# Feature-major units of a streamed gated block: 512-column products with the high weights, halves added when a unit leaves PSUM

## The chip, the core and the metric

One core of a Trainium2 chip runs the whole program. Its engines are PE (TensorE, matrix products), DVE (VectorE), ACT (ScalarE), POOL (GpSimd) and SP (SyncE, which here only issues transfers); 16 DMA engines move data between device memory and SBUF. Matrix results land in PSUM. The metric is the device time of one execution in microseconds (us), less is better.

## The reference

All arrays are float32. `x` is [1, 256, 2048]: 256 tokens with 2048 features; the branches are W = 1024 wide.

```python
h = rmsnorm(x, norm_pre)
(q_a, f_a, i_a, z_a, u_b, z_b, rkvwa_c, z_c, xbc_d, dt_d, z_d, gate_pre) = h @ w_in   # [2048, 21648]
o_a = hgrn2(q_a, f_a, i_a) * silu(z_a)
o_b = s5(u_b, ...) * silu(z_b)          # ends with g * sigmoid(g @ w_glu + b_glu), g = gelu(y)
o_c = rwkv7(token_shift(rkvwa_c), ...) * silu(z_c)
o_d = mamba2(conv4(xbc_d), dt_d, z_d)   # causal convolution over 4 tokens, per channel; silu(z) inside
merged = sum(sigmoid(gate_pre[b] + gate_bias[b]) * (o[b] @ w_up[b]) for b in range(4))
out = x + rmsnorm(merged @ w_out, norm_post)
```

The token shift is `xs + mu * (previous token's xs - xs)`. Each branch holds a recurrence over the 256 tokens (S5's is a complex scan per state). The work is mostly the three large products with `w_in`, `w_up` and `w_out`.

## The kernel before

**The stream.** The weights of all large products pass through the core once, in 444 chunks of 128 x 1024 elements (512 KB). A chunk is loaded as `raw` by a transfer on SP's queue (three raw buffers), then split in two parts of the reduced type fp32r: `hi` is a rounded copy made by ACT, `lo` is `raw - hi`, made by DVE (four buffers of each). A product of two float32 matrices is then three products of parts: high by high, high by low and low by high. The normalised input `h` lies transposed as eight tiles `h0` to `h7`; for one k tile (128 features of the contraction) there are 512 columns, 0:256 the high part of the 256 tokens and 256:512 their low part. The split of a chunk runs three chunks ahead of its products.

**Units.** A unit is a set of chunks that fill one PSUM tile `pg` of [128, 2, 512], of which there are two. In a feature-major unit (kind "fm") a 128 x 128 weight tile is the stationary operand and `h` moves past it: the result has features on the partitions and 256 tokens in a row, two feature tiles `f` to a unit. Each k tile and feature tile takes three products of 256 columns, `hi` with the high part, `hi` with the low part, `lo` with the high part, all added into the same 256 columns `ps[:, f, 0:256]`. In a token-major unit (kind "tm") the activations are stationary and 512 columns of weights move; the change does not touch it. Feature-major are `u` (chunks 0 to 15), dt (16, 17), the convolution's input xBC (18 to 49), the two low-rank inputs (50, 51), k, r, v (52 to 99), q, f (100 to 131), z of the RWKV branch (212 to 227) and of S5 (324 to 339), and the glu product of S5 (380 to 387, whose moving operand `ghl` is S5's own result). The gates, up projections and the output (388 to 443) are token-major.

**Evacuation.** When a unit's last products are issued, a generator (`shift_done`, `conv_done`, `plain_done`, `u_done`, `zfm_done`, `glu_done`, `dt_done`) takes the result out of PSUM in stages: for the token shift ACT copies the tile scaled by `mu` to `evm` and DVE combines `pg` with it; for the convolution ACT scales the tile once and DVE adds three shifted multiples of it, six reads of `pg` in all; `plain_done` (q, f) is one copy on ACT and a store on ACT's queue.

**The order.** Each engine works through its instructions in the order in which the program emits them, fixed when it is built. `_Stream.loop` emits, for each step, a split, a load, one chunk's products, stages of evacuations, and then as many stages of branch work ("jobs": S5's tiles `s50` to `s57`, the halves of HGRN, RWKV's and Mamba's steps) as fit. How many fit is settled by an estimate: each helper (`mm`, `act`, `tt`, `stt`, `ts`) books a cost on its engine's clock (`t_pe`, `t_act`, `t_dve`), and `run_jobs` goes on

```python
        while max(K.t_dve, K.t_act) <= K.t_pe + AHEAD:
```

with AHEAD = 3.7 us. A stage of a job comes only after the estimate has its last stage finished (`can`). If a unit needs a job that is not done when its products are due, `products` calls `finish`, which emits the rest of that job in one go, ahead of the unit. The glu units need job "b" (gelu of S5's early tiles read back) and "s57", S5's last tile, which has two halves; in a half, DVE computes a phase `ph`, ACT its sine and cosine `cs5`, PE the input products `pb`, DVE the rotated inputs `ta`, four scans and the products `ta`, `tb` with the cosines, and PE the output products.

**The start.** `prologue` holds x in tiles of 128 tokens by 1024 features (`x00`, `x01` the first 128 tokens, `x10`, `x11` the others), scales them by the rows' norms in pieces of 512 features, transposes them on PE into `pb` banks, and DVE and ACT write `h0` to `h7`. Products of the first two chunks (`j < 2`) come by part, as far as `h` is there.

Of the kernel before, what the change touches and what calls it, by code (L numbers as in the profile page):

```python
# [60 lines left out]
PE_GAP = 0.0  # L61
# [5 lines left out]
# the functions that each activation table serves  # L67
# [6 lines left out]
class _Kern:  # L74
    """Pools, constants and instruction helpers shared by the weight stream and the branches."""

    def __init__(self, ctx, tc, drams):
# [20 lines left out]
        self.soft = False  # L98
        self.o = {}
# [23 lines left out]
    def wait(self, n):  # L123
        """Until n more slots are free."""
# [5 lines left out]
    def wait_banks(self, n):  # L130
        """Until n more PSUM banks are free."""
# [5 lines left out]
    def fm(self, name, n=2):  # L137
        """A feature-major [128, 4 n, 256] array, in tiles of four feature tiles."""
# [23 lines left out]
    def book(self, engine, cost, out, ins):  # L162
        """Book an instruction: it starts when the engine is free and its operands are there."""
# [31 lines left out]
    def act(self, out, in_, func, **kw):  # L195
# [7 lines left out]
        ins = [in_] + [x for x in (kw.get("scale"), kw.get("bias")) if hasattr(x, "tensor")]  # L203
        self.book("t_act", cost, out, ins)
# [4 lines left out]
    def _dve(self, out, ins, ns):  # L209
        """Book a vector instruction; one that reads the last one's output waits for it."""  # L210
        self.book("t_dve", 0.06 + ns * 1e-3, out, ins)
# [15 lines left out]
    def stt(self, out, in0, scalar, in1, op0, op1, **kw):  # L227
        self._dve(out, (in0, in1), self._n(out) * 1.045)
        return self.nc.vector.scalar_tensor_tensor(out=out, in0=in0, scalar=scalar, in1=in1, op0=op0, op1=op1, **kw)  # L229

    def ts(self, out, in0, s1, s2, op0, op1=None):
        self._dve(out, (in0,), self._n(out) * 0.53)
# [21 lines left out]
    def mm(self, out, lhsT, rhs, start=True, stop=True, **kw):  # L254
        n = self._n(rhs)
        if rhs.dtype == F32R:
            cost = n * 0.427e-3 if n >= 256 else n * 1.67e-3
        else:
            cost = max(n * 1.67e-3 * min(out.shape[0], 128) / 128, 0.027)
        self.book("t_pe", cost + PE_GAP * (1 if rhs.dtype == F32R else 2), out, (lhsT, rhs))  # L260
        return self.nc.tensor.matmul(out, lhsT, rhs, start=start, stop=stop, **kw)  # L261

    def tr(self, out, in_, b=0):
        """out = in_ transposed; in_ starts at partition b."""
# [12 lines left out]
    def ld(self, out, in_):  # L277
        """A transfer whose source may still be under way."""
# [3 lines left out]
    def ldx(self, out, in_):  # L282
        """A load of what has long been in DRAM."""
# [5 lines left out]
    def st(self, out, in_):  # L289
        """A store of what the scalar engine has just written."""  # L290
# [11 lines left out]
    def split(self, hi, lo, src):  # L302
        """src (float32 in SBUF) as the exact sum of two float32r parts."""
# [3 lines left out]
    def rstd(self, out, ss, n, eps):  # L307
        """out = 1 / sqrt(ss / n + eps), small tiles."""
# [1980 lines left out]
```

## Time and profile before

| what | value |
|---|---|
| runs | 1427.38, 1429.43, 1424.73 us; median 1427.38 |
| the profiled execution | span 1427.8 us from the first to the last instruction, taken as its time |
| mean granted TensorE clock | 0.993 of full speed |
| busy, share of the span | PE 97%, PE's weight loads 86%, DVE 73%, ACT 58%, POOL 11% |
| transfers | 288.62 MB, 202 GB/s over the span |
| matmul records | 9751 |
| largest groups | splits `lo` on DVE, 444 of 1223 ns; splits `hi` on ACT, 444 of 1055 ns; feature-major products on PE, 2624 with `hi` and 1312 with `lo`; token-major products, 1408 with `hi` and 704 with `lo` against `h` |

The busy time of PE is that of pipelined products, whose durations overlap: the mean of one can be twice the pace at which they follow each other. The pace is read from a stretch of the chain of waits in which PE waits for nothing. The rows `pg<-h,hi` and `pg<-h,lo` are the feature-major products, `pg<-hi,h` and `pg<-lo,h` the token-major ones, since the stationary operand is named last.

### The profile page before, as it was taken

The page shows a single profiled execution, that of the slowest core. Times are in us where ns is not written, and L with a number is a line of the kernel's source. Part 1 is how long each engine was busy: PE and PEld are TensorE (multiplying, and loading weights), DVE is VectorE, ACT ScalarE, POOL GpSimd, SP SyncE. Part 2 cuts the span into 40 slices and gives each one's busy share as a digit, 9 for nine tenths or more (in the row PEclk, how much of TensorE's full clock was granted, in tenths as well). Part 3 has the DMA queues.
Part 4 walks back from the last instruction along what each step waited for, and adds up shares of the span by engine and source line. Part 5 has one row for each costly group of instructions (what it writes and reads, how often), then busy time and mean ns, then how long its engine had stood idle before and what let it go on. Part 6 is the DMA issues. An engine that isn't in the chain of part 4 may idle for free.

```text
span 1427.8 us, 24645 instructions
## 1 busy us (share of the span) xinstructions
PE 1390.9 (97%) x9751; PEld 1223.2 (86%) x9751; DVE 1038.0 (73%) x1422; ACT 827.1 (58%) x1136; POOL 162.0 (11%) x268
## 2 busy tenths in 40 slices
PE   8999989989999999999999999999999999999997
PEld 7999989989989887888789888888789987888886
DVE  6787488778786784576787699767978788576655
ACT  5455445845456546765578765787556444544442
POOL 6232310010025320011100001000010000000000
PEclk9999999999999999999999999999999999999999
DMA  7878985487657876477876567655686856676664
GB/s 214 239 240 263 279 270 163 135 191 232 206 155 175 228 236 179 142 203 201 232 207 198 181 207 197 211 177 172 193 197 194 214 177 191 213 267 194 183 195 135
DMA packets 199040, 288.62 MB, mean 202 GB/s; under 512 B 12453, under 2 KB 116750, under 8 KB 198926
## 3 DMA queue, kind: packets, MB, share of 16 engines
q1 hardware_dynamic: 169614, 237.15, 54.2%
q0 software_dynamic: 25216, 43.05, 13.9%
q10 hardware_dynamic: 4096, 6.86, 1.4%
q8 instruction: 76, 1.25, 0.3%
q14 instruction: 38, 0.31, 0.1%
HBM read 268.33 MB, written 18.66 MB: 201 GB/s over the span
## 4 chain that ended last, share of the span: by engine, by line
PE 71%; DMA 8%; DVE 8%; issue 6%; ACT 6%; POOL 0%; SPq 0%; ACTq 0%; DVEq 0%; POOLq 0%
PE pg L261 63%; PE pb L261 6%; DMA raw<-in_w_in_dram 6%; DVE lo L216 4%; ACT hi L207 2%; PE pb L267 1%; DVE ta L216 1%; ACT L207 1%; DMA cn<-in_s_c_im_dram 1%; DMA x<-in_x_dram 1%; DVE invtmp L216 0%; ACT hT L207 0%; DVE tb L243 0%; DVE tb L216 0%; DMA ds5b<-bl 0%
## 5 line engine op out<-in xcount | busy, mean ns | idle before, releaser
L216 DVE TENSOR_TENSOR lo<-raw,hi 128x1024 fp32r<-128x1024 f32 x444 | 541.1, 1223 | 350.6 <-ACT hi L207 342.3
L207 ACT ACTIVATE hi<-raw 128x1024 fp32r<-128x1024 f32 x444 | 465.9, 1055 | 532.7 <-PE pg L261 249.1
L261 PE MATMUL pg<-h,hi 128*128 128x256 f32 x2624 | 480.8, 286 | 4.1 <-DVE ev L229 3.6
L261 PE MATMUL pg<-hi,h 128*128 128x512 f32 x1408 | 448.1, 393 | 0.1
L261 PEld LDWEIGHTS pg<-h,hi 128*128 128x128 f32 x2624 | 409.9, 192 | 10.7 <-issue 6.9
L261 PE MATMUL pg<-h,lo 128*128 128x256 f32 x1312 | 371.6, 285 | 5.0 <-DVE lo L216 4.1
L261 PEld LDWEIGHTS pg<-hi,h 128*128 128x128 f32 x1408 | 264.9, 188 | 58.5 <-issue 2.5
L261 PE MATMUL pg<-lo,h 128*128 128x512 f32 x704 | 275.5, 391 | 2.6 <-DVE lo L216 2.4
L261 PEld LDWEIGHTS pg<-h,lo 128*128 128x128 f32 x1312 | 251.0, 192 | 6.7 <-DVE lo L216 5.4
L261 PE MATMUL pg<-hi,o 128*128 128x512 f32 x512 | 164.2, 394 | 0.0
L261 PEld LDWEIGHTS pg<-lo,h 128*128 128x128 f32 x704 | 132.6, 188 | 30.5 <-DVE lo L216 4.5
L261 PEld LDWEIGHTS pg<-hi,o 128*128 128x128 f32 x512 | 96.1, 188 | 21.9 <-issue 1.6
L261 PE MATMUL pg<-lo,o 128*128 128x512 f32 x256 | 99.8, 390 | 0.0
L261 PE MATMUL pg<-hi,mhl 128*128 128x512 f32 x224 | 71.1, 391 | 0.0
L280 POOL DMA_DIRECT2D gb<-in_gate_bias_dram x16 | 8.7, 545 | 541.1 <-DVE gate L216 477.9
L207 ACT ACT_TABLE_LOAD x51 | 65.4, 1283 | 5.3 <-DVE mss L235 2.8
L261 PEld LDWEIGHTS pg<-lo,o 128*128 128x128 f32 x256 | 48.1, 188 | 9.5
L261 PEld LDWEIGHTS pg<-hi,mhl 128*128 128x128 f32 x224 | 42.1, 188 | 8.7
L261 PE MATMUL pg<-lo,mhl 128*128 128x512 f32 x112 | 43.6, 389 | 0.0
L243 DVE TENSOR_TENSOR_SCAN tb<-s5p,ta 128x256 f32<-128x256 f32 x64 | 41.7, 701 | 0.1
L261 PEld LDWEIGHTS pg<-lo,mhl 128*128 128x128 f32 x112 | 21.0, 188 | 4.2
L261 PE MATMUL pg<-ghl,hi 128*128 128x256 f32 x128 | 23.1, 283 | 0.0
(371 smaller groups left out, 1362.6 us busy)
## 6 DMA issues: line engine op xcount, KB each, us to landing
raw<-in_w_in_dram SPq DMA_DIRECT2D x340, 512.0 KB
raw<-in_w_up_dram SPq DMA_DIRECT2D x64, 512.0 KB
raw<-in_w_out_dram SPq DMA_DIRECT2D x32, 512.0 KB
us<-duhl POOLq DMA_DIRECT2D x16, 256.0 KB, 6.4
bs<-ds5b POOLq DMA_DIRECT2D x16, 256.0 KB, 7.6
gb<-in_gate_bias_dram POOLq DMA_DIRECT2D x16, 256.0 KB, 4.7
raw<-in_s_w_glu_dram SPq DMA_DIRECT2D x8, 512.0 KB
x<-in_x_dram SPq DMA_DIRECT2D x4, 512.0 KB
```

The costliest lines, as they stand in the source:

```text
L207: return self.nc.scalar.activation(out=out, in_=in_, func=func, **kw)
L216: return self.nc.vector.tensor_tensor(out=out, in0=in0, in1=in1, op=op)
L243: return self.nc.vector.tensor_tensor_scan(out=out, data0=data0, data1=data1, initial=0.0, op0=ALU.mult, op1=ALU.add)
L261: return self.nc.tensor.matmul(out, lhsT, rhs, start=start, stop=stop, **kw)
L267: return self.nc.tensor.transpose(out, in_, self.ident[b:b + p, b:b + p])
L280: return self.nc.gpsimd.dma_start(out=out, in_=in_)
```

## The change

1. In feature-major units `hi` multiplies both parts of `h` in one product of 512 columns, into all of `ps[:, f, 0:512]`: the high-by-high sum in columns 0:256, the high-by-low sum in 256:512. `lo` with the high part stays a product of 256 columns into 0:256. Of a unit's last k tile, `lo` comes first and `hi` ends the accumulation.
2. The first two chunks keep three products of 256 columns, with the high-by-low sum in 256:512. Those columns are set to zero by a memset on DVE ahead of chunk 0's products.
3. A new helper `join` adds the halves: ACT copies columns 256:512 to SBUF, DVE adds columns 0:256. All evacuations of feature-major units begin with it and then read the joined tile (`dt_done` has the same pair of its own). The store of q and f moves from ACT's queue to POOL's.
4. The estimate's costs change: a product costs 0.0133 us and 0.417 ns a column (before 0.427 ns a column), a change between full and partial tiles 0.15 us, an operand passed by pointer 0.09 on ACT and 0.065 on DVE.
5. `load_g` waits until S5's early tiles are done. Comments and docstrings go, so line numbers shift (`mm`'s instruction from L261 to L270, DVE's `tt` from L216 to L220, `act` from L207 to L210).

```diff
@@ act, _dve, stt, ts
+        cost += POINTER_ACT * (len(ins) - 1)
...
-        self.book("t_dve", 0.06 + ns * 1e-3, out, ins)
+        ptr = sum(hasattr(x, "tensor") for x in scalars)
+        self.book("t_dve", 0.06 + ns * 1e-3 + POINTER_DVE * ptr, out, ins)
@@ mm
-            cost = n * 0.427e-3 if n >= 256 else n * 1.67e-3
+            cost = n * 0.417e-3 + 0.0133 if n >= 256 else n * 1.67e-3
...
-        self.book("t_pe", cost + PE_GAP * (1 if rhs.dtype == F32R else 2), out, (lhsT, rhs))
+        parted = out.shape[0] < 128 or lhsT.shape[0] < 128
+        if parted != self.parted:
+            self.parted = parted
+            cost += 0.15
+        self.book("t_pe", cost, out, (lhsT, rhs))
@@ products
-                u.ps = u.ps[:, 0:u.nc_ // 128, 0:256]
+                u.ps = u.ps[:, 0:u.nc_ // 128, :]
...
         elif j < 2:
+            if c == 0:
+                K.nc.vector.memset(ps[:, :, 256:512], 0.0)
...
-                        K.mm(ps[:, f, :], w[:, kk, 128 * f:128 * f + 128], u.mv(k)[:, z:z + 256],
+                        K.mm(ps[:, f, z:z + 256], w[:, kk, 128 * f:128 * f + 128], u.mv(k)[:, z:z + 256],
...
-                    K.mm(ps[0:u.cols or 128, f, :], hi[:, kk, fs], m[:, 0:256], start=first, stop=False)
-                    K.mm(ps[0:u.cols or 128, f, :], hi[:, kk, fs], m[:, 256:512], start=False, stop=False)
-                    K.mm(ps[0:u.cols or 128, f, :], lo[:, kk, fs], m[:, 0:256], start=False, stop=last)
+                    pf = ps[0:u.cols or 128, f, :]
+                    if not last:
+                        K.mm(pf, hi[:, kk, fs], m, start=first, stop=False, skip_group_check=True)
+                    K.mm(pf[:, 0:256], lo[:, kk, fs], m[:, 0:256], start=False, stop=False, skip_group_check=True)
+                    if last:
+                        K.mm(pf, hi[:, kk, fs], m, start=False, stop=True, skip_group_check=True)
@@ new
+    def join(ps, name="ev"):
+        t = K.big([128, ps.shape[1], 256], name=name)
+        t = t[0:ps.shape[0]]
+        K.act(t, ps[:, :, 256:512], AF.Copy)
+        K.add(t, ps[:, :, 0:256], t)
+        return t
@@ shift_done
+            s = join(ps)
+            yield 0
...
-                K.act(m[:, f, 1:257], ps[:, f, :], AF.Copy, scale=K.par("mu", f0 + f))
+                K.act(m[:, f, 1:257], s[:, f, :], AF.Copy, scale=K.par("mu", f0 + f))
@@ plain_done
-            K.act(ev, ps, AF.Copy)
-            K.st(spilled[key][:, i0:i0 + 2], ev)
+            K.ld(spilled[key][:, i0:i0 + 2], join(ps))
@@ load_g
+        while f"s5{S5_EARLY - 1}" not in S.done:
+            yield 1
```

Three places of the fixed order. A name is a tile with its running numbers; `x2` means twice in a row.

**The start, DVE.** Between the splits `lo1` and `lo2` of chunks 1 and 2. Before:

```order
L216 TENSOR_TENSOR lo1_224<-raw1_106,hi1_223 128x1024
L229 SCALAR_TENSOR_TENSOR h2_3_79<-pb_24_213,npc_147,h2_3_79 128x256 x2
L229 SCALAR_TENSOR_TENSOR h3_4_80<-pb_25_218,npc_147,h3_4_80 128x256 x2
L234 TENSOR_SCALAR x11_12_88<-x11_12_88,xrs_16_125 128x512
L229 SCALAR_TENSOR_TENSOR h4_5_81<-pb_27_270,npc_147,h4_5_81 128x256 x2
L216 TENSOR_TENSOR lo2_285<-raw2_108,hi2_284 128x1024
```

Now:

```order
L220 TENSOR_TENSOR lo1_224<-raw1_106,hi1_223 128x1024
L233 SCALAR_TENSOR_TENSOR h2_3_79<-pb_24_213,npc_147,h2_3_79 128x256 x2
L233 SCALAR_TENSOR_TENSOR h3_4_80<-pb_25_218,npc_147,h3_4_80 128x256 x2
L238 TENSOR_SCALAR x11_12_88<-x11_12_88,xrs_16_125 128x512
L1641 MEMSET pg26_245 128x2x256
L233 SCALAR_TENSOR_TENSOR h4_5_81<-pb_27_271,npc_147,h4_5_81 128x256 x2
L220 TENSOR_TENSOR lo2_286<-raw2_108,hi2_285 128x1024
```

The memset of the first unit's PSUM tile stands behind the second scaling of x, and PE's first product of that tile, which waited for ACT's part of `h0` and `hi0` alone, now waits for the memset too.

**Ahead of the glu units, PE.** Before, the last output products of S5's last tile (`pb_610`) stand between chunks 369 and 370, and chunk 380, the first with `ghl`, follows chunk 379 directly:

```order
L261 MATMUL pg606_12342<-hi369_12386,h5_6_82 128x512
L261 MATMUL pb_610_12462<-ta_608_12357,cu_588_11901 32x256 x2
L261 MATMUL pb_610_12462<-tb_609_12358,cu_588_11901 32x256 x4
L261 MATMUL pb_610_12462<-ta_608_12357,cu_588_11901 32x256 x2
L261 MATMUL pg606_12342<-hi370_12406,h6_7_83 128x512
...
L261 MATMUL pg612_12519<-lo379_12591,h7_8_84 128x512
L261 MATMUL pg612_12519<-hi379_12590,h7_8_84 128x512
L261 MATMUL pg614_12668<-ghl_560_11190,hi380_12608 128x256 x2
L261 MATMUL pg614_12668<-ghl_560_11190,lo380_12609 128x256
```

Now:

```order
L270 MATMUL pg617_11237<-lo379_11331,h7_8_84 128x512
L270 MATMUL pg617_11237<-hi379_11330,h7_8_84 128x512
L270 MATMUL pb_627_11432<-us_610_11138,bs_611_11139 128x256 x2
L270 MATMUL pb_628_11435<-us_610_11138,bs_611_11139 128x256 x2
L270 MATMUL pb_631_11452<-ta_629_11438,cu_612_11144 32x256 x2
L270 MATMUL pb_631_11452<-tb_630_11439,cu_612_11144 32x256 x4
L270 MATMUL pb_631_11452<-ta_629_11438,cu_612_11144 32x256 x2
L270 MATMUL pg632_11466<-ghl_572_10262,hi380_11349 128x512
L270 MATMUL pg632_11466<-ghl_572_10262,lo380_11350 128x256
```

The input products (`pb_627`, `pb_628`) and the output products (`pb_631`) of the tile's second half now stand between the two chunks, with no other product among them.

**The same place, DVE.** Before, the work of that half tile is spread among the splits of chunks 365 to 371:

```order
L234 TENSOR_SCALAR ph_602_12284<-ph_602_12284 128x512
L229 SCALAR_TENSOR_TENSOR ph_602_12284<-ph_602_12284 128x512
L216 TENSOR_TENSOR lo366_12308<-raw366_12267,hi366_12307 128x1024
...
L216 TENSOR_TENSOR lo369_12387<-raw369_12338,hi369_12386 128x1024
L243 SCALAR_TENSOR_TENSOR tb_609_12358<-s5p_32_442,ta_608_12357 128x256 x2
L216 TENSOR_TENSOR lo370_12407<-raw370_12369,hi370_12406 128x1024
L216 TENSOR_TENSOR ta_608_12357<-tb_609_12358,cs5_601_12283 128x1024
L216 TENSOR_TENSOR tb_609_12358<-tb_609_12358,cs5_601_12283 128x1024
L216 TENSOR_TENSOR lo371_12427<-raw371_12390,hi371_12426 128x1024
```

Now:

```order
L220 TENSOR_TENSOR lo383_11419<-raw383_11371,hi383_11418 128x1024
L220 TENSOR_TENSOR gate_626_11424<-pg617_11237,gb_616_11235 128x1024
L238 TENSOR_SCALAR ph_625_11415<-ph_625_11415 128x512
L233 SCALAR_TENSOR_TENSOR ph_625_11415<-ph_625_11415 128x512
L220 TENSOR_TENSOR ta_629_11438<-pb_627_11432,cs5_624_11414 128x512
...
L220 TENSOR_TENSOR ta_629_11438<-ta_629_11438,tb_630_11439 128x2x256 x2
L247 SCALAR_TENSOR_TENSOR tb_630_11439<-s5p_32_435,ta_629_11438 128x256 x4
L220 TENSOR_TENSOR ta_629_11438<-tb_630_11439,cs5_624_11414 128x1024
L220 TENSOR_TENSOR tb_630_11439<-tb_630_11439,cs5_624_11414 128x1024
L233 SCALAR_TENSOR_TENSOR cu_612_11144<-cu_612_11144,pt_115,pb_631_11452 64x256
```

The half tile now comes in one piece behind the split of chunk 383 and a gate's addition, with no split among its rows.

**One evacuation of v, DVE.** Before, and then now:

```order
L1833 MEMSET evm_213_4232 128x2
L229 SCALAR_TENSOR_TENSOR ev_212_4231<-pg199_4044,omu_423,evm_213_4232 128x256 x2
L216 TENSOR_TENSOR lo100_4240<-raw100_4168,hi100_4239 128x1024
```

```order
L220 TENSOR_TENSOR ev_197_3329<-pg193_3201,ev_197_3329 128x512
L1857 MEMSET evm_198_3332 128x2
L233 SCALAR_TENSOR_TENSOR ev_197_3329<-ev_197_3329,omu_416,evm_198_3332 128x256 x2
L220 TENSOR_TENSOR lo100_3340<-raw100_3284,hi100_3339 128x1024
```

The join's addition comes first and is the last read of `pg`; the combination reads the joined tile.

More of the change, by code (lines that the diff above doesn't have):

```diff
@@ L60 @@
 LATENCY = 0.12
-PE_GAP = 0.0
+POINTER_ACT = 0.09
+POINTER_DVE = 0.065
 DMA_RATE = 220e3
@@ L98, in __init__ @@
         self.soft = False
+        self.parted = False
         self.o = {}
@@ L207, in act, with _dve @@
         return self.nc.scalar.activation(out=out, in_=in_, func=func, **kw)
-    def _dve(self, out, ins, ns):
-        self.book("t_dve", 0.06 + ns * 1e-3, out, ins)
+    def _dve(self, out, ins, ns, scalars=()):
+        ptr = sum(hasattr(x, "tensor") for x in scalars)
+        self.book("t_dve", 0.06 + ns * 1e-3 + POINTER_DVE * ptr, out, ins)
         self.last = out.tensor
@@ L227, in stt @@
     def stt(self, out, in0, scalar, in1, op0, op1, **kw):
-        self._dve(out, (in0, in1), self._n(out) * 1.045)
+        self._dve(out, (in0, in1), self._n(out) * 1.045, (scalar,))
         return self.nc.vector.scalar_tensor_tensor(out=out, in0=in0, scalar=scalar, in1=in1, op0=op0, op1=op1, **kw)
     def ts(self, out, in0, s1, s2, op0, op1=None):
-        self._dve(out, (in0,), self._n(out) * 0.53)
+        self._dve(out, (in0,), self._n(out) * 0.53, (s1, s2))
         if op1 is None:
@@ L1634, in products @@
                     for f in range(u.nc_ // 128):
-                        K.mm(ps[:, f, :], w[:, kk, 128 * f:128 * f + 128], u.mv(k)[:, z:z + 256],
-                             start=(k == 0 and n == 0), stop=False)
+                        K.mm(ps[:, f, z:z + 256], w[:, kk, 128 * f:128 * f + 128], u.mv(k)[:, z:z + 256],
+                             start=(k == 0 and n == 0), stop=False, skip_group_check=True)
         else:
@@ L1834, in done @@
             for f in range(nf):
[L1835 removed]
+                K.act(m[:, f, 1:257], s[:, f, :], AF.Copy, scale=K.par("mu", f0 + f))
             yield 0
             for f in range(nf):
[L1838 to L1839 removed]
+                if dst in spilled:
+                    o = s[:, f, :]
                 else:
                     o = dst() if i0 is None else dst()[i0 // 4][:, i0 % 4 + f, :]
[L1842 to L1844 removed]
+                K.stt(o, s[:, f, :], K.omu[:, f0 + f:f0 + f + 1], m[:, f, 0:256], ALU.mult, ALU.add)
+            if dst in spilled:
+                K.ld(spilled[dst][:, i0:i0 + 2], s)
             if then:
@@ L1863, in done @@
         def done(ps):
+            s = join(ps, "evs")
+            yield 0
             t = K.big([128, 2, 256], name="ev")
@@ L1891, in done @@
         def done(ps):
-            ev = K.big([128, 2, 256], name="ev")
+            ev = join(ps)
             hl = K.big([128, 2, 2, 256], F32R, name="uhl")
-            K.act(hl[:, 0], ps, AF.Copy)
-            K.act(ev, ps, AF.Copy)
+            K.act(hl[:, 0], ev, AF.Copy)
             K.st(spilled["u"][:, i0:i0 + 2], ev)
@@ L1929, in done @@
         def done(ps):
-            zs = K.big([128, 2, 256], name="zs")
             yield 0
-            K.act(zs, ps, AF.Silu)
+            zs = join(ps, "zs")
+            yield 0
+            K.act(zs, zs, AF.Silu)
             def post():
@@ L2025, in done @@
         def done(ps):
-            ev = K.big([128, 2, 256], name="ev")
+            ev = join(ps)
+            yield 0
             for f in range(2):
-                K.act(ev[:, f, :], ps[:, f, :], AF.Sigmoid, bias=K.par("b_glu", 2 * j + f))
+                K.act(ev[:, f, :], ev[:, f, :], AF.Sigmoid, bias=K.par("b_glu", 2 * j + f))
             def post():
```

15 lines of the change are left out of this document (5 added, 10 removed).

## The prediction, made before the changed kernel ran

> **What bounds the kernel now.** I read the page's engine totals first, then the chain that ended last, then the two calmest stretches of that chain in order of time.
>
> ```profile
> PE 1390.9 (97%) x9751; PEld 1223.2 (86%) x9751; DVE 1038.0 (73%) x1422; ACT 827.1 (58%) x1136; POOL 162.0 (11%) x268
> PE 71%; DMA 8%; DVE 8%; issue 6%; ACT 6%; POOL 0%; SPq 0%; ACTq 0%; DVEq 0%; POOLq 0%
> 325.53 75.06 PE pg L261 x624
> 1343.29 55.11 PE pg L261 x243
> ```
>
> TensorE holds 71% of the chain, so time taken off its products should come off the end, except where another engine or a transfer holds the chain. The two pieces give the true pace, which the busy time does not (its durations overlap): 624 products of 256 columns in 75.06 us are 120.3 ns each, 243 of 512 columns in 55.11 us are 226.8 ns. Twice the columns cost 106.5 ns more, so one product costs 0.416 ns a column and 13.8 ns besides.
>
> **The product.** A feature-major unit now needs, per weight tile, one 512-column and one 256-column product instead of three of 256: 226.8 + 120.3 = 347.1 against 360.9 ns, 13.8 ns less.
>
> ```profile
> L261 PE MATMUL pg<-h,lo x1312: 276/283/580, 15.3 to 1126.3; 128*128 128x256 f32 x186, 128*16 128x256 f32 x2
> L261 PE MATMUL pg<-ghl,lo x64: 283/283/283, 1240.3 to 1263.0; 128*128 128x256 f32 x64
> ```
>
> Each low-part product stands for one triple: 1312 + 64, less the 16 of the first two chunks, which keep three products, are 1360. 1360 x 13.8 ns = **18.8 us** less, the ceiling of the gain. The Trainium skill prices a warm product lower: its page "TensorE: Matmul & The Clock Gate", section "Back-to-back issue gap", gives N/2.4 + 2.5 ns, so a product fewer would save 2.5 ns, 3.4 us in all as an estimate from that page. The rows above, 13.8 ns on both sizes, decide against it; I keep it as a rival.
>
> Not all of the 18.8 us lies on the path. The chain's early part:
>
> ```profile
> 14.56 2.87 PE pg L261 x24
> ...
> 25.48 1.13 DVE lo L216
> 26.64 6.38 DMA raw<-in_w_in_dram
> 35.47 8.84 DMA raw<-in_w_in_dram
> ...
> 73.40 6.93 DMA raw<-in_w_in_dram
> ```
>
> From 26.64 to 80.33 us the chain goes through raw weight transfers (five in the answer, first, second and last shown), so faster products only wait longer. At 2.88 us a chunk (24 x 120 ns) the 66 us from 14.3 to 80.3 are 22 chunks of 8 triples, two of them without a gain: 160 x 13.8 ns = **2.2 us** not realised. Bounds: 0, and 3.6 if the transfers rule up to chunk 33.
>
> **The zeroing at the start.** By the order, the first product now waits for DVE's memset, which stands behind the second scaling of x. The rows of before:
>
> ```profile
> 0.97 0.38 DVE L325 MEMSET prow<- 128x384 f32 x1 [0.97 <-PEq L2275]
> 14.31 1.19 PE L261 MATMUL pg<-h,hi 128*128 128x256 f32 x8
> 18.38 0.47 DVE L234 TENSOR_SCALAR x<-x,xrs 128x512 f32<-128x512 f32 x1
> ```
>
> That scaling ends at 18.85; a memset of 512 elements, by the row of 384, takes 0.38 x 512/384 = 0.51 us. So the first product starts at 19.3 instead of 14.31, 5.0 us later. Behind it on PE stand the transposes that DVE needs for the next part of h; behind those on DVE stands the split of chunk 2, which frees the raw buffer of chunk 5. The chain shows this path: the first products, a split, a raw transfer. I take **+5.0 us**. Below, 1: later transfers share the queues with fewer others. Above, 6.7, with the slow clock:
>
> ```profile
> 314.45 0.58 PE L261 MATMUL pg<-h,lo 128*128 128x256 f32 x1 [2.17 <-DVE lo L216]
> 314.00:317.40 3.40, 2.95 (x14) 2.95 (x15) 3.40 (x4) 1.08 (x2) 0.00 (x0) 0.54 1.04 322
> ```
>
> After a wait of 2.17 us the granted clock was 0.54 over 3.4 us, and the window holds 14 products where 25 would fit at 120 ns; some 3 us of it ran at half pace and lost half, 1.7 us with the edges.
>
> **The S5 half tile before the gate units.** The glu units (chunks 380 to 387) need S5's last tile. Before, its last products stood after chunk 369, ten chunks ahead. Now PE's order puts its input products, its output products and then chunk 380 behind chunk 379 with nothing in between; on DVE the half tile stands behind the split of chunk 383 and a gate's addition. That split cannot start until the products of 379 are done, since there are four hi buffers. So PE waits for a serial chain, priced by before's rows for the same instructions:
>
> ```profile
> 1191.80 0.42 DVE L234 TENSOR_SCALAR ph<-ph 128x512 f32<-128x512 f32 x1
> 1192.26 0.69 DVE L229 SCALAR_TENSOR_TENSOR ph<-ph 128x512 f32<-128x512 f32 x1
> 1193.25 0.61 ACT L207 ACTIVATE ph<-ph 128x512 f32<-128x512 f32 x1
> 1194.29 0.71 ACT L207 ACTIVATE cs<-ph,halfpi 128x512 f32<-128x512 f32 x1
> 1194.97 0.47 PE pb L261 x4
> 1198.50 0.68 DVE L216 TENSOR_TENSOR ta<-pb,cs 128x512 f32<-128x512 f32 x1
> 1201.01 1.29 DVE L216 TENSOR_TENSOR ta<-ta,tb 128x512 f32<-128x512 f32 x2
> 1203.36 1.26 DVE L243 TENSOR_TENSOR_SCAN tb<-s5p,ta 128x256 f32<-128x256 f32 x2
> 1207.95 1.22 DVE L216 TENSOR_TENSOR ta<-tb,cs 128x1024 f32<-128x1024 f32 x1
> 1209.20 1.22 DVE L216 TENSOR_TENSOR tb<-tb,cs 128x1024 f32<-128x1024 f32 x1
> 1211.79 1.00 PE pb L261 x16
> 1240.09 0.40 PE L261 MATMUL pg<-ghl,hi 128*128 128x256 f32 x2
> 1240.29 1.06 ACT L207 ACTIVATE hi<-raw 128x1024 fp32r<-128x1024 f32 x1 [1.66 <-PE pg L261]
> 1241.39 1.23 DVE L216 TENSOR_TENSOR lo<-raw,hi 128x1024 fp32r<-128x1024 f32 x1 [1.49 <-ACT hi L207]
> 1242.53 1.22 DVE L216 TENSOR_TENSOR gate<-pg,gb 128x1024 f32<-128x1024 f32 x1
> ```
>
> From 1240.09, when the glu products could begin: split and gate end 3.7 us later (1243.75). Then ph 1.15 (0.46 to the second row, and its 0.69), the three ACT rows 1.75 (1193.25 to 1195.00), ta and tb with their sums 3.80 (1198.50 to 1202.30), two pairs of scans 2.52, two products with the cosines and sines 2.47 (1207.95 to 1210.42), PE's output products 1.00: 16.4 us. The half tile's own 0.47 + 1.00 of PE were paid elsewhere before, so 14.9 are new; with one slow stretch of 1.7, **+16.6 us**. Bounds: 11.2, if the split and the gate were already past; 18.3, with two slow stretches. Behind the waiting products on PE stands the stream itself; DVE and ACT only run out of work.
>
> **The joins.** 45 evacuations gain a copy on ACT and an addition on DVE, each waiting for the other engine; the eight plain units gain the addition alone and move their store to POOL, where a row of 0.5 to 0.6 us on an engine busy 11% costs nothing unless an S5 load queues behind it.
>
> ```profile
> L207 ACT ACTIVATE ev<-pg x14: 581/589/1007, 34.6 to 514.7; 128x512 f32<-128x512 f32 x12, 128x1024 f32<-128x1024 f32 x2
> L216 DVE TENSOR_TENSOR ta<-pb,cs 128x512 f32<-128x512 f32 x32 | 21.8, 683 | 0.1
> 118.00:466.00 348.00, 334.25 (x2899) 322.80 (x2898) 256.42 (x395) 195.88 (x284) 54.76 (x69) 0.98 0.74 205
> 732.00:780.00 48.00, 48.00 (x406) 47.21 (x405) 40.52 (x51) 38.95 (x47) 0.00 (x0) 1.00 0.61 189
> ```
>
> A join is 0.59 on ACT and 0.68 on DVE. DVE is busy 256 of 348 us in the long stretch, and the cover is that slack plus the splits' lead of three chunks; the run of 624 products above had evacuations in it and no wait. In the four z units from 732 DVE would go from 40.5 to 43.2 of 46.3 us, so little cover is left there. Bounds: 0, and 8 us (some twelve units in crowded stretches at 0.68). I take **+2.0**, nearer to the quiet run.
>
> A gain stands against it. The bank is free after the join, no longer after conv's six reads:
>
> ```profile
> PE pg L261 <- DVE ev L229: 3.6, 1, 3.6
> PE pb L267 <- DVE cx L235: 2.1, 1, 2.1
> ```
>
> The first wait may go, 3.6 us and a slow stretch, 5.3 at most; but DVE's join stands behind the same late split, so I take **-2.0** and keep 0 to -5.3.
>
> The estimate's new paces cost nothing themselves but move S5's and RWKV's work some 10 to 30 chunks later up to chunk 130, about 15 from there on. Other waits move with it, such as the second row; I set their sum at 0, within 6 either way (twice a wait of 2.1 with its slow stretch is 7.6).
>
> Sum: -18.8 + 2.2 + 5.0 + 16.6 + 2.0 - 2.0 = +5.0 us. The profiled execution's span was 1427.8, with nothing around it that the times show; the median of the three runs is 0.4 below it. So 1427.4 + 5.0 = **1432.4 us**. Three runs spread over 4.7 us, so 0.3% (4.3 us) is about what can be told from no change.
>
> **Rivals.**
> - *The old waits vanish (faster).* The moved work no longer meets the places where PE waited: 5.3 at the conv evacuation, 3.8 at cx (2.1 and a slow stretch), 3.9 at 314.45 (2.17 and its stretch): 13.0, against the 2.0 counted, gives 1421.4. Faster from 9.3 us of the 11 on. For it: after 800 us of the chain such waits are rare. Against: the same kinds of work meet the stream elsewhere.
> - *The joins crowd DVE (slower still).* If 20 units pay the addition and as long a wait for ACT, 20 x (0.68 + 0.59) = 25, less overlap a half: 12.7 instead of 2.0, so 1443. It decides where DVE's share passes 90%, as in the z units; the quiet run speaks against it.
> - *The gain is not there.* If the 13.8 ns were nothing that a saved product saves, only about 3 us would come off: 1432.4 + 15.4 = 1448. The page's 2.5 ns above would give the same; the two pieces of the chain speak against it. Or the transfers hold the chain up to chunk 131: 110 chunks more x 8 x 13.8 ns = 12.1, 1444.5; yet in 75 us from 325 no transfer is on the chain.
>
> **How the numbers follow.** The forecast has 0.62, its own range 1425 to 1439; rival one 0.18, rival two 0.12, rival three 0.08. Faster: 0.16 of rival one and 0.02 of the forecast, 0.18. Within 0.3% (1423.1 to 1431.7): 0.27 of the forecast and 0.02, 0.29. Slower: 0.33 and the last two rivals, 0.53. The range 1419 to 1444 leaves out the ends of rival one and most of rival three.
>
> **What would show it.** PE's products in feature-major units at 347 ns a pair; the first of them at 19.3 us with a wait for DVE's memset; a wait of some 15 us before the first glu product, ending on DVE's tb, with a slow clock behind it; DVE share above 0.85 in the z units. The forecast fails if that wait is under 8 us, if the start is made up by chunk 34, or if waits of over 2 us turn up in crowded stretches that had none.

## The result and the profile after

The changed kernel takes 1473.3 us (median; 1469.1 to 1481.8) against 1427.4 before: a ratio of 1.033, interval 1.030 to 1.037. The forecast was 1432.4, within 1419 to 1444. The profiled execution is its quickest, 1469.1 us, with a span of 1467.4. (The time is 1.7 us longer than the span; the forecast saw nothing around the span, but its sum does not rest on that.)

The engine totals and the granted clock of the changed kernel:

```profile
PE 1395.4 (95%) x8391; PEld 1153.9 (79%) x8391; DVE 1069.4 (73%) x1469; ACT 848.2 (58%) x1172; POOL 167.2 (11%) x276
core 0: 1467.4 us, clock 0.979
```

1360 products fewer, and PE is busy longer, at a lower clock: what 0.979 leaves of 1467.4 us is 30.8 us, partly while PE waited; what 0.993 left of 1427.8 was 10.0. To see where the time went, the span is cut at the same chunks in both kernels: from the first product to chunk 132, then to 164, 212, 228, 276, 356, 380 and the end. Before (start:end, length, busy time with instruction counts of PE, its weight loads, DVE, ACT and POOL, then clock, DMA share and GB/s):

```profile
14.30:466.20 451.90, 435.30 (x3730) 421.31 (x3729) 340.77 (x588) 250.94 (x363) 88.80 (x127) 0.98 0.76 211
466.20:567.50 101.30, 98.64 (x679) 81.43 (x678) 72.55 (x117) 53.95 (x77) 20.42 (x27) 0.98 0.77 218
567.50:732.40 164.90, 162.12 (x1257) 130.77 (x1256) 107.55 (x121) 106.95 (x160) 15.94 (x26) 1.00 0.72 199
732.40:780.20 47.80, 47.80 (x406) 47.06 (x405) 40.73 (x51) 38.55 (x47) 0.00 (x0) 1.00 0.61 188
780.20:928.00 147.80, 147.80 (x889) 121.00 (x889) 117.83 (x136) 97.46 (x133) 9.86 (x17) 1.00 0.65 198
928.00:1171.80 243.80, 243.69 (x1526) 206.74 (x1525) 189.59 (x220) 156.04 (x207) 10.28 (x17) 1.00 0.67 188
1171.80:1240.10 68.30, 68.30 (x326) 55.20 (x325) 50.36 (x54) 31.95 (x34) 1.08 (x2) 1.00 0.66 207
1240.10:1427.80 187.70, 179.37 (x897) 152.14 (x895) 112.74 (x122) 83.38 (x104) 3.71 (x7) 0.99 0.62 195
```

After:

```profile
19.80:438.80 419.00, 406.09 (x2468) 349.79 (x2468) 314.67 (x557) 226.39 (x323) 56.40 (x88) 0.98 0.74 217
438.80:562.90 124.10, 111.55 (x590) 86.18 (x589) 92.31 (x128) 67.24 (x96) 38.56 (x37) 0.93 0.62 165
562.90:737.20 174.30, 170.57 (x1493) 139.41 (x1493) 99.03 (x114) 103.84 (x159) 22.84 (x36) 0.97 0.66 188
737.20:791.80 54.60, 50.35 (x273) 42.09 (x273) 37.52 (x41) 33.61 (x47) 3.81 (x6) 0.97 0.83 210
791.80:944.80 153.00, 150.31 (x910) 121.77 (x909) 128.25 (x154) 111.39 (x150) 8.83 (x15) 1.00 0.67 200
944.80:1188.00 243.20, 243.20 (x1415) 200.14 (x1414) 204.35 (x245) 168.93 (x222) 11.33 (x19) 1.00 0.66 189
1188.00:1278.60 90.60, 74.84 (x365) 57.17 (x363) 68.50 (x81) 41.43 (x48) 5.42 (x9) 0.93 0.66 181
1278.60:1467.40 188.80, 179.28 (x834) 148.68 (x832) 113.65 (x127) 84.32 (x108) 3.16 (x6) 0.99 0.55 187
```

The changed kernel starts 5.5 us late, is 27.4 us ahead at chunk 132 (438.8 against 466.2), and then loses: 22.8 up to chunk 164, 9.4, 6.8 and 5.2 in the next three stretches, 22.3 in the three gates ahead of the glu units. The sum, 5.5 - 32.9 + 22.8 + 9.4 + 6.8 + 5.2 - 0.6 + 22.3 + 1.1, is 39.6, the difference of the spans; the medians differ by 45.9, since the quickest execution was profiled. The rows with a clock under 1.00 hold stretches of half clock, most of them behind waits of PE.

Part of the lead at chunk 132 is work put off: up to there PE did 562 products into `pb` banks, nearly all of them branch work, before (48.9 us of busy time) and 339 (31.1 us) after; from chunk 132 to 212 it did 972 (39.1 us) before and 1122 (52.4 us) after. The rest of the loss in that second stretch is mostly waits and the slow clock behind them.

The three largest groups of PE's waits (sum, times, longest):

```profile
PE pb L270 <- DVE ta L220: 19.6, 2, 14.2
PE pg L270 <- DVE lo L220: 9.6, 9, 4.9
PE pg L270 <- DVE pg L1641: 4.9, 1, 4.9
```

The third is the start, as forecast; the timeline shows DVE's memset and PE's first product behind it:

```profile
19.13 0.48 DVE L1641 MEMSET pg<- 128x512 f32 x1
19.76 1.62 PE L270 MATMUL pg<-h,hi 128*128 128x256 f32 x6 [4.95 <-DVE pg L1641]
```

The 14.2 us are the half tile of S5 ahead of the glu units: the last product of its own input, its first output product 14.16 us later, and the window from the one to the next:

```profile
1260.81 0.40 PE L270 MATMUL pb<-us,bs 128*128 128x256 f32 x2
1275.60 1.07 PE L270 MATMUL pb<-ta,cu 128*32 128x256 f32 x4 [14.16 <-DVE ta L220]
1261.20:1279.00 17.80, 3.54 (x20) 1.20 (x19) 13.58 (x20) 5.16 (x6) 0.54 (x1) 0.62 0.32 104
```

Before, PE had no wait in those three gates. The clock was at 0.62 over those 17.8 us. The Trainium skill, "TensorE: Matmul & The Clock Gate", section "Part 1: The HAM clock gate", says that the gate halves the clock after an idle window of about 3.4 us. The stretches of half clock here have that length or a multiple of it, but a shorter wait can be enough, and the measurement decides: before, one followed a wait of 2.17 us, and in the changed kernel one followed a wait of 1.4 us (at 494 us) and one a wait of 1.8 us (at 590 us).

### The profile page after: what moved, and what is told of

It is laid out like the page before. It is cut to its first block, busy times and chain, and to the rows that moved or that the text cites. A ratio compares the mean times of both kernels' runs of the same rounds, so it can differ in the third digit from the quotient of the medians.

```text
span 1467.4 us, 22081 instructions
## 1 busy us (share of the span) xinstructions
PE 1395.4 (95%) x8391; PEld 1153.9 (79%) x8391; DVE 1069.4 (73%) x1469; ACT 848.2 (58%) x1172; POOL 167.2 (11%) x276
## 4 chain that ended last, share of the span: by engine, by line
PE 38%; DVE 11%; DMA 7%; ACT 5%; issue 5%; DVEq 0%; ACTq 0%; POOLq 0%
PE pg L270 33%; PE pb L270 5%; DMA raw<-in_w_in_dram 5%; DVE lo L220 4%; ACT hi L210 2%; DMA raw<-in_w_up_dram 1%; DVE ta L220 1%; DVE E L220 1%; DVE tb L247 1%; DVE invtmp L220 1%; DMA XA<-dab 1%; PE pb L276 1%; ACT L210 1%; DVE tb L220 0%; DVE XT L220 0%
## 5 line engine op out<-in xcount | busy, mean ns | idle before, releaser
L220 DVE TENSOR_TENSOR lo<-raw,hi 128x1024 fp32r<-128x1024 f32 x444 | 541.2, 1226 | 331.2 <-ACT hi L210 328.2
L210 ACT ACTIVATE hi<-raw 128x1024 fp32r<-128x1024 f32 x444 | 462.4, 1053 | 456.1 <-PE pg L270 215.8
L270 PE MATMUL pg<-h,hi 128*128 128x512 f32 (+2 forms) x1328 | 467.8, 399 | 9.5 <-DVE pg L1641 4.9
L270 PE MATMUL pg<-hi,h 128*128 128x512 f32 x1408 | 453.2, 396 | 0.0
L270 PE MATMUL pg<-h,lo 128*128 128x256 f32 x1312 | 362.0, 283 | 3.4 <-DVE lo L220 3.2
L270 PEld LDWEIGHTS pg<-hi,h 128*128 128x128 f32 x1408 | 266.5, 189 | 61.4 <-issue 3.7
L270 PEld LDWEIGHTS pg<-h,hi 128*128 128x128 f32 (+1 forms) x1328 | 246.8, 189 | 68.6 <-issue 6.3
L270 PE MATMUL pg<-lo,h 128*128 128x512 f32 x704 | 276.9, 393 | 6.4 <-DVE lo L220 6.4
L270 PEld LDWEIGHTS pg<-h,lo 128*128 128x128 f32 x1312 | 247.7, 190 | 9.9 <-DVE lo L220 6.2
L270 PE MATMUL pg<-hi,o 128*128 128x512 f32 x512 | 167.0, 400 | 0.0
L270 PEld LDWEIGHTS pg<-lo,h 128*128 128x128 f32 x704 | 133.4, 189 | 34.0 <-DVE lo L220 7.8
L270 PEld LDWEIGHTS pg<-hi,o 128*128 128x128 f32 x512 | 98.1, 192 | 22.7 <-issue 1.2
L270 PE MATMUL pg<-lo,o 128*128 128x512 f32 x256 | 101.5, 396 | 0.0
L270 PE MATMUL pg<-hi,mhl 128*128 128x512 f32 x224 | 71.0, 391 | 0.0
L270 PEld LDWEIGHTS pg<-lo,o 128*128 128x128 f32 x256 | 49.1, 192 | 9.8
L270 PEld LDWEIGHTS pg<-hi,mhl 128*128 128x128 f32 x224 | 42.0, 188 | 8.6
L270 PE MATMUL pg<-lo,mhl 128*128 128x512 f32 x112 | 43.6, 389 | 0.0
L270 PE MATMUL pb<-ta,cu 128*32 128x256 f32 x128 | 19.7, 416 | 19.6 <-DVE ta L220 19.6
L270 PEld LDWEIGHTS pb<-ta,cu 128*32 128x32 f32 x128 | 6.5, 115 | 25.4 <-issue 23.9
```

The source lines that it names most:

```text
L210: return self.nc.scalar.activation(out=out, in_=in_, func=func, **kw)
L220: return self.nc.vector.tensor_tensor(out=out, in0=in0, in1=in1, op=op)
```

## The experiments

The questions: do the joins cost the time (the rival "the joins crowd DVE"), the places of the branch work, the new costs of the estimate, or the half tile alone? Medians follow; before ran beside them at 1426.1 to 1429.7.

**e1: new products and joins, branch work in its old places.** The costs are the old ones, a pair books what three products booked, and `join` restores the clocks:

```diff
+        now = K.t_act, K.t_dve
...
         K.act(t, ps[:, :, 256:512], AF.Copy)
         K.add(t, ps[:, :, 0:256], t)
+        K.t_act, K.t_dve = now
...
```

> The changed kernel with all its products and joins, but the estimate books a pair of products as the three of before, the joins not at all, and everything else at the old costs: the branch work keeps the places that it had before (S5's last products behind chunk 367, before 369, changed 379). Placement theory (the changed kernel loses 46 us because moved branch work makes PE wait, and PE's clock halves behind each wait): 1427.4 - 18.8 + 5.5 (start) + 1.7 (its slow clock) + 2 (joins) = about 1418, between 1412 and 1424. Joins theory (the added copies and additions delay the splits): 1440 or more, with waits for lo in it. Estimate theory says the same as placement here.

1454.1 us, ratio 1.020 (1.015 to 1.024), in the joins theory's range. On PE the branch products stand within three chunks of where the kernel before has them. The old places take away 19 us, not the 55 of the placement theory; e5 below tells whether the joins are the rest. One wait in it shows the mechanism. ACT's rows around a join of a z unit, in the kernel before (where the silu reads PSUM itself):

```profile
781.25 0.58 ACT L207 ACTIVATE zs<-pg 128x512 f32<-128x512 f32 x1
781.72 3.29 ACT L207 ACTIVATE hT<-hT,lb 128x256 f32<-128x256 f32 x8
...
787.30 2.94 ACT L207 ACTIVATE hi<-raw 128x1024 fp32r<-128x1024 f32 x3
```

The same place in e1, and PE's wait there:

```profile
798.73 0.58 ACT L210 ACTIVATE zs<-pg 128x512 f32<-128x512 f32 x1
802.74 0.63 ACT L210 ACTIVATE zs<-zs 128x512 f32<-128x512 f32 x1 [3.43 <-DVE zs L220]
803.28 3.29 ACT L210 ACTIVATE hT<-hT,lb 128x256 f32<-128x256 f32 x8
...
808.84 2.93 ACT L210 ACTIVATE hi<-raw 128x1024 fp32r<-128x1024 f32 x3
809.93 0.49 PE L270 MATMUL pg<-hi,h 128*128 128x512 f32 x1 [3.81 <-ACT hi L210]
```

The copy is as quick as the silu was. But the silu behind it must wait 3.43 us for DVE's addition, which stands behind a split and two steps of S5 on DVE, and with it waits everything behind it on ACT: the next `hi` comes 10.1 us after the unit's first read instead of 6.05, and PE stands for 3.81.

**e2: the new costs alone**, on the kernel before:

```diff
-            cost = n * 0.427e-3 if n >= 256 else n * 1.67e-3
+            cost = n * 0.417e-3 + 0.0133 if n >= 256 else n * 1.67e-3
```

(and the costs of pointers and of partial tiles).

> The kernel before with only the new costs in the estimate; products and evacuations are those of before. S5's last products come behind chunk 342, so there is no forced half tile. Estimate theory (the new costs are what makes the order bad): slower by 15 to 30 us, 1442 to 1457. Placement theory: the order changes without the half tile; other waits come and go, 1427 within 8.

1484.5 us, ratio 1.040 (1.036 to 1.044). PE, DVE and POOL have as many instructions as before and ACT four more (table loads); only the places differ, and 57 us are lost. That is twice what the estimate theory gave.

**e3: the changed kernel with the old costs**, the same lines the other way round.

> The changed kernel with the old costs in the estimate; joins and pairs booked by them. S5's last products still stand behind chunk 379. Estimate theory: the middle of the program recovers and the half tile stays, about 1450. Placement theory: another bad order of the same sort, 1460 to 1485. Joins theory: 1465 to 1475.

1569.9 us, ratio 1.098 (1.093 to 1.104). All theories missed. Taking the new costs out does not mend the changed kernel: without them it is 97 us slower still. This moves the branch work once more, so it does not tell what the new costs do with the places held.

**e4: the last gate unit ahead of glu.**

```diff
-    for j in range(3):
+    for j in range(4):
         gate_unit(1, j)
...
-    gate_unit(1, 3)
```

> The changed kernel with the last gate unit (8 chunks) ahead of the glu units, so that S5's last half tile is spread over those chunks; everything ahead of it is the same. If the half tile's chain (14.4 us of wait and 6.9 of half clock) is all that the place costs: 1473 - 21 + 3 (a short rest of the chain, the last addition, gelu and split) = 1455, between 1450 and 1460. If the wait only moves to the next unit: 1465 or more.

1477.1 us, ratio 1.033 (1.027 to 1.039): nothing gained, as the second theory had it. The wait of 14.2 us ahead of glu is gone, and these come between the glu units and the up projections, which had the gate between them before:

```profile
PE pg L270 <- DVE o L220: 5.7, 3, 2.6
PE pg L270 <- ACT ghl L210: 3.9, 1, 3.9
PE pg L270 <- ACT o L210: 1.7, 1, 1.7
```

**e5: e1 without the joins.**

```diff
-            s = join(ps)
+            s = ps[:, :, 0:256]
```

(and likewise in each evacuation).

> The kernel of e1_old_work_order (new products, branch work in the old places) without the joins: the evacuations are those of before and read columns 0:256 alone, so the high-by-low sum is left out of the result. Joins theory (the joins' round trip between ACT and DVE makes the splits late; by the stretches of e1 they cost 20 us up to chunk 131 and 7 in the z units): 1454 - 25 = 1429, between 1424 and 1434. If the joins were as cheap as forecast (2 us): 1452, and the loss of e1 would lie in the products or the start.

1429.5 us, ratio 1.001 (1.000 to 1.003): with the branch work in its old places the joins cost 1454.1 - 1429.5 = 24.6 us, as expected from e1's stretches.

**e6: e1 with three products.** The accumulation is changed: each half of a bank is opened by a start of its own, so the sums differ.

```diff
+                    K.mm(pf[:, 0:256], hi[:, kk, fs], m[:, 0:256], start=first, stop=False, skip_group_check=True)
+                    K.mm(pf[:, 256:512], hi[:, kk, fs], m[:, 256:512], start=first, stop=False, skip_group_check=True)
+                    K.mm(pf[:, 0:256], lo[:, kk, fs], m[:, 0:256], start=False, stop=last, skip_group_check=True)
```

> The kernel of e1 with its joins and places, but three products of 256 columns again, the high-by-low one into columns 256:512; the estimate books them as the pair. Price as forecast, 13.8 ns on 1360 products, all on the path: 1454 + 18.8 = 1473. Pace as seen in many units of the changed kernel (353 instead of 347 ns a pair) and part of it hidden in waits: 1454 + 8 to 13 = 1462 to 1467. No price: 1454.

1453.9 us, ratio 1.018 (1.016 to 1.020): no difference to e1 that can be told, as the expectation "no price" had it. In the profiles (e6's is its slowest execution, e1's its quickest) e6 takes 448.1 us from the second unit to chunk 132 and e1 441.4, so there the pair does save something. Three units with no wait in e6, and the same three in e1 and in e5:

```profile
381.00:415.60 34.60, 34.60 (x290) 34.60 (x290) 30.96 (x57) 14.91 (x21) 1.62 (x3) 1.00 0.73 219
378.00:411.90 33.90, 33.90 (x194) 29.45 (x193) 31.01 (x57) 14.93 (x21) 1.63 (x3) 1.00 0.73 225
363.30:397.20 33.90, 33.90 (x193) 29.45 (x192) 27.30 (x49) 14.92 (x21) 0.00 (x0) 1.00 0.75 226
```

96 triples in 34.6 us are 360 ns each, 96 pairs in 33.9 us 353: half of the forecast saving. Two stretches of the changed kernel, of three units and of one:

```profile
126.90:160.80 33.90, 33.90 (x194) 29.42 (x193) 24.70 (x37) 18.38 (x24) 0.00 (x0) 1.00 0.67 212
46.30:57.40 11.10, 11.10 (x65) 9.78 (x64) 9.46 (x30) 4.92 (x6) 2.74 (x4) 1.00 0.81 228
```

There are two paces: 96 pairs in 33.9 us again, and 32 in 11.1, the 347 ns of the forecast. Most units run at 353 (two thirds of the chunks that have no branch product in them). What decides between them stays open.

**e7: old products, branch work copied to the changed kernel's places**, by a list of which job's stage is emitted at which chunk:

```diff
-        while max(K.t_dve, K.t_act) <= K.t_pe + AHEAD:
+        for name in PLAN.get(self.step, ()):
```

> The kernel before (products, evacuations, start) with its branch work put chunk by chunk where the changed kernel has it, S5's last half tile behind chunk 379 included. Placement theory: the places alone cost what separates the changed kernel from e1, 1473 - 1454 = 19, of which 21 is the half tile: 1446, between 1440 and 1452. If the places only hurt together with joins: 1427 + 16 to 21 for the half tile alone would not hold, under 1440. If the old products suffer more in these places: over 1455.

1484.1 us, ratio 1.039 (1.038 to 1.041), which is the last theory's range. But S5 found less room for its tiles here, its last tile came a chunk late, and both of its halves landed behind chunk 379 instead of one; so its loss there (a wait of 17.6 us and another of 10.5 behind it) is not the changed kernel's. Up to chunk 356 the places agree within a chunk, and there it is 14.8 us behind the kernel before (1186.6 against 1171.8 us), the changed kernel 16.2. From chunk 132 to 164 its waits are those of the changed kernel, in the products of before:

```profile
PE pb L298 <- DVE ta L253: 5.5, 1, 5.5
PE pg L298 <- DVE lo L253: 5.0, 1, 5.0
```

The stretch itself is as long as the changed kernel's, 124.5 us against 124.1:

```profile
432.80:557.30 124.50, 111.73 (x590) 86.41 (x589) 93.91 (x127) 67.17 (x95) 38.80 (x36) 0.93 0.62 164
```

So these waits come from the places, not from products or joins.

**e8: e1 with the joined tile read a chunk later.**

```diff
             s = join(ps)
-            yield 0
+            yield 1
```

(so in the evacuations with the shift, the convolution, u and z; the branch work is held in its old places by a list, as in e7).

> The kernel of e1 with the rest of an evacuation (the reads of the joined tile on ACT) put one chunk behind its join, so that ACT's queue no longer waits for DVE's addition ahead of the next split. If that wait is what the joins cost: 10 to 20 us back, 1434 to 1444. If it is the work itself on DVE and ACT, or the later freeing of PSUM: 1450 to 1458.

1435.8 us, ratio 1.006 (1.004 to 1.008): 18.3 of the 24.6 us come back, with the same instructions but for one table load on ACT. The place of e1's wait now:

```profile
778.12 0.58 ACT L246 ACTIVATE zs<-pg 128x512 f32<-128x512 f32 x1
778.59 3.30 ACT L246 ACTIVATE hT<-hT,lb 128x256 f32<-128x256 f32 x8
...
784.17 1.04 ACT L246 ACTIVATE hi<-raw 128x1024 fp32r<-128x1024 f32 x1
```

`hi` follows 6.05 us behind the copy, as before the change. That ACT waits in its queue for DVE's addition is therefore shown as the larger part of what the joins cost there.

**e9: e8 with the memset at the very start of DVE's queue.**

```diff
+    K.pg0 = K.psg.tile([128, 2, 512], F32, tag="pg", name="pg0")
+    nc.vector.memset(K.pg0[:, :, 256:512], 0.0)
     S.prepare()
...
```

> The kernel of e8_join_a_step_ahead with the first unit's PSUM tile set to zero at the very start of DVE's queue, before x has come, so that the first product no longer waits for the memset. In e8 that product started 5.3 us late and PE's clock was halved for 6.8 us behind it. If the start is worth what was forecast (5.0, at most 6.7): 1435.8 - 5 to 7 = 1429 to 1431. If the raw transfers make up for it by chunk 34: 1434 or more.

1430.2 us, ratio 1.002 (1.000 to 1.004): 5.5 us less than e8, against the forecast's 5.0 (the two intervals overlap by a little). By the medians the raw transfers did not make up for it. The two profiles leave it open: e9 is 6.3 us ahead of e8 at chunk 16, 2.1 at chunk 52 and level at chunk 164, but e8's is the quickest of its executions and e9's one of its slowest.

**e10: the kernel before with pairs only from chunk 100 on**, the silu of z a chunk behind its join. The main line:

```diff
-                u.ps = u.ps[:, 0:u.nc_ // 128, 0:256]
+                u.ps = u.ps[:, 0:u.nc_ // 128, :] if j >= PAIRS else u.ps[:, 0:u.nc_ // 128, 0:256]
```

> The kernel before, its branch work in its own places, with the pair of products only from chunk 100 on (q, f, both feature-major z groups, glu; 18 units), joins not booked, the silu of z one chunk behind its join; u, xBC and k, r, v keep three products and their evacuations, and there is no memset. By the stretches of e8: 2.6 us less in q and f, 2.0 in the z units, 0.6 in glu, so 1428 - 5 = 1423, between 1420 and 1426. If the joins cost there what they cost up to chunk 100: 1428 or more.

1429.2 us, ratio 1.002 (1.000 to 1.003): no gain. In the profile it is 1.8 us ahead at chunk 276 and loses 5.5 between there and glu (317.6 against 312.1), where S5's last tile had come two chunks earlier than in the kernel before.

**e11: the changed kernel with S5's last tiles spread**, so that its last output products stand behind chunk 376.

```diff
-        return job.ready <= self.step and job.stamp <= self.K.t_pe + SLACK
+        return job.ready <= self.step and job.stamp <= self.K.t_pe + SLACK + (2.0 if self.step >= 311 and job.name in ("s55", "s56", "s57") else 0.0)
```

> The changed kernel with one number of its order changed: from chunk 311 on the stages of S5's last three tiles may follow each other more closely, so that the last output products stand behind chunk 376 and not in one piece behind 379. Up to chunk 335 the order is that of the changed kernel. If the half tile's wait (14.4 us) and the slow clock behind it (6.9) are a loss of their own: 1473 - 21 + 1 = 1453, between 1449 and 1458. If the waits only move into the gate units ahead: 1465 or more.

1469.3 us, ratio 1.029 (1.026 to 1.032): 4 us of the 21, and the interval overlaps the changed kernel's (1.030 to 1.037). Its stretches from chunk 324 to 356 and from there to glu:

```profile
1103.70:1203.70 100.00, 95.65 (x515) 78.46 (x514) 82.83 (x102) 54.51 (x71) 8.63 (x14) 1.00 0.73 194
1203.70:1279.00 75.30, 72.00 (x346) 56.47 (x346) 60.48 (x70) 37.88 (x44) 1.08 (x2) 1.00 0.60 189
```

The gates ahead of glu take 75.3 instead of 90.6, the eight units ahead of them 100.0 instead of 92.3: half of what the gates lost moved there. The rest of what is missing lies ahead of chunk 324, where nearly all of the order is the same and this execution was 8.0 us later (1103.7 against 1095.7): waits of one order differ between executions, and differences under some 8 us between two profiles mean little.

**e12: the kernel before with pairs in all units but chunks 16 to 51**, memset first, reads a chunk behind the join, and PE's branch products exactly in their old places.

> The kernel before with its branch work exactly in its own places on PE, the first unit's tile set to zero at the very start, and the pair of products in all feature-major units but dt, xBC and the low-rank inputs (chunks 16 to 51), which keep three products and their evacuations; joins not booked, the reads of a joined tile one chunk behind the join. By the quiet units of e5 and e9 a unit saves 0.2 to 0.3 us: 32 units of 8 chunks' worth give 6 to 10 us: 1427 - 8 = 1419, between 1416 and 1422. If the joins cost as much as the pairs save even there: 1425 to 1430, as in e10. If they cost more than that: over 1430.

1425.9 us against 1428.0, ratio 0.998 (0.996 to 0.999). Faster, but by a quarter of what was expected, and in the range of the second theory, by which the joins cost about what the pairs save. In the profile, 3.6 us of gain is there at the last unit, 6.4 at chunk 132. The edit is that of e10 with `THREE[0] <= j < THREE[1]` for the chunks that keep three products, and e9's.

**e13: e5 in the places of the changed kernel**, S5's end as in e7.

> The new products without the joins (as e5, the high-by-low sum is left out), with the branch work in the places of the changed kernel up to chunk 347; from there S5 comes a chunk later and its whole last tile stands behind chunk 379, as in e7. Read up to chunk 356, the first gate of S5 (changed kernel 1188.0 us in its profile, e7 with the old products 1186.6, old places 1171.8): if the joins cost in these places what they cost in the old ones, 25 us, it is reached at 1163 to 1168; if these places bring their own waits and the joins add only 4 or 5 (e7 to changed: 1.4 later, of it 5.5 the start and some 11 less by the products), at 1181 to 1185. The time of the whole: about 1475 to 1480 with the second, 1460 with the first.

1483.7 us, ratio 1.037 (1.034 to 1.040). Chunk 356 begins at 1192.5 us, against 1188.0 with the joins: the 25 us that the joins cost in the old places are not there, and the first expectation (1163 to 1168) falls. The second (1181 to 1185) is missed by 8 us to the other side. How much the joins cost in these places is not shown closely: this execution is the slowest of its four by 6 us, and the changed kernel's is the quickest of its four.

**The runs side by side.** The lengths of the stretches in us, in the profiled executions, from the first product to chunk 132 and on between the same chunks (the late start itself is not in them):

| kernel | places | products, joins | to 132 | to 164 | to 212 | to 228 | to 276 | to 356 | sum |
|---|---|---|---|---|---|---|---|---|---|
| before | old | three, none | 451.9 | 101.3 | 164.9 | 47.8 | 147.8 | 243.8 | 1157.5 |
| e5 | old | pair, none | 444.8 | 102.3 | 165.3 | 46.9 | 147.9 | 244.4 | 1151.6 |
| e1 | old | pair, joins | 456.9 | 103.1 | 166.0 | 47.3 | 154.5 | 243.4 | 1171.2 |
| e7 | new | three, none | 418.6 | 124.5 | 174.4 | 50.0 | 160.3 | 244.6 | 1172.4 |
| e13 | new | pair, none | 421.6 | 125.2 | 173.9 | 49.3 | 159.7 | 243.2 | 1172.9 |
| changed | new | pair, joins | 419.0 | 124.1 | 174.3 | 54.6 | 153.0 | 243.2 | 1168.2 |

The places set the shape of a row. In all three kernels with the new places PE waits at the same chunks: 5.5 us at 138, 1.4 at 144, 4.9 to 5.8 at 154. The new places alone cost 14.9 us up to chunk 356 (e7 against before), the joins alone 19.6 (e1 against e5). Together they do not cost both: with pairs and joins the new places cost nothing more up to there (changed against e1), and in the new places the joins cost nothing that the profiles show (changed against e13).

## Why the prediction was wrong

Up to chunk 356 the forecast's terms come to -10.7 us: the sum of 5.0 without the half tile's 16.6 is -11.6, and 0.9 of that belongs to the glu units behind. Measured were +16.2 (1188.0 against 1171.8). From there to the glu units the forecast had 16.6, and 22.3 were measured. So the larger error, 27 us, lies in the first part.

- **The step that failed first: other waits, "their sum at 0, within 6 either way".** Up to chunk 356 the moved work alone cost 14.8 us (e7: old products, no joins, old start). It made the first 132 chunks quicker (451.9 to 418.6 us in e7, 419.0 in the changed kernel), in part because work was only put off, and then met the stream at chunks 132 to 212, where PE waited at places that had no wait. The row at chunk 132 to 164, 101.3 to 124.1, is the forecast's "waits of over 2 us" turning up in stretches that had none. The bound of 6 was taken from waits of one good order; e2 (57 us over before) and e7 (57) show what another order of the same work can cost here. The move was also larger than the forecast read it. Most branch products stand some 15 chunks later, but S5's output products 10 to 78 (the first behind chunk 133 instead of 61). And the reason given for it was wrong: in e2 the new costs alone end S5 at chunk 342 instead of 369, earlier than before. The old costs with joins booked and pairs booked as they are (e3) still end it at 379, and with the joins not booked and a pair booked as three products the old places are back (e1); so one of these two bookings or both push it back.
- **The joins: +2.0 forecast, 24.6 in the old places (e1 against e5).** The forecast priced instructions (0.59 on ACT, 0.68 on DVE) and looked for DVE at its limit, above 0.85 in the z units; DVE's share at chunk 212 to 228 is 37.5 of 54.6 us. What costs is ACT's queue standing for DVE's (e8: 18.3 of it). In the new places a cost of the joins is not seen (e13), though a few us may be there. Why the two losses do not add up stays open; so no run splits the changed kernel's 46 us between them.
- **The product: -18.8 + 2.2 forecast, -10.8 measured at best.** In the old places without joins (e5 against before, without the start): 429.3 against 437.8 from the second unit to chunk 132, 0.9 and 0.8 in the z units, 0.6 in glu. A pair saves 7 ns in most units instead of 13.8. In the new places even this is not seen: 405.2 us (e13) and 403.8 (changed) against 404.5 with three products (e7).
- **The start: right.** 4.95 us of wait at 19.76 (forecast 5.0 at 19.3), 5.5 in e9.
- **The half tile: right in mechanism and place, and near in the wait** (14.16 us, forecast as 14.9; it ends on DVE's `ta`, which the first output products read, and not on `tb`). The stretch lost 22.3 against 16.6, since more than the half tile stands in it: the branch products on PE are busy 8.6 us there instead of 2.8, and `lo` is waited for twice, 1.5 us. The half rate lasted 13.7 us, but mostly while PE waited; about 3 us of it lie behind the wait, so the forecast's 1.7 for it stands (and the 6.9 in the expectations of e4 and e11 was too much). And it is no price that can be taken away alone (e4, e11).
- **The gain of 2.0 from an earlier free bank** is there at its place, the wait ahead of chunk 52: 3.6 us before, and then in e5 (without joins) and in e1 (with them):

```profile
PE pg L270 <- DVE ev L233: 4.5, 1, 4.5
PE pg L270 <- DVE evs L220: 1.5, 1, 1.5
```

  But e1 has a new wait of 3.5 us for a join's `ev` at chunk 18, so nothing is left of the gain in the sum.

Of the rivals, "the old waits vanish" had the moved work, with the wrong sign: it holds up to chunk 132 and is reversed behind it. "The joins crowd DVE" came nearest in its direction; its mechanism and its place were other ones. The measured time lies above every rival's: none let the moved work cost anything.

## What to carry to other kernels

When an order was built by an estimate, a change that alters booked costs is two changes: the work, and the places of everything else. Hold the order fixed while the first is measured, and give the second a wide range of its own, mostly upwards. Two losses that were each measured alone need not add up. An evacuation that goes from ACT to DVE and back should have other work between its steps: an in-order queue that waits for its partner delays what is behind it, and the price is the next split, not the added instruction.

## What the runs showed of the hardware

The same pair of products of 512 and 256 columns runs at 347 ns in some units and at 353 in most, for a unit at a time and with no wait in it. Stretches of half clock came in lengths of 3.4, 6.8 and 13.7 us in the changed kernel (and one of 6.3 at its end). Most followed a wait of PE, of 1.1 to 14.2 us, but the length of the wait alone does not decide: one of 2.0 us at 299 us was followed by none. The one of 6.8 us from 603 us on followed no wait over 0.15 us, but 128 products of 32x32 that took PE 4.4 us.
